# Plain fp32 products in a Hyena convolution, and other homes, later sums and longer lags around it

## The chip, the cores and the metric

The kernel runs on one core of a Trainium2 chip. The metric is the device time of one execution in microseconds (us), the median of three runs. The profile is of one execution more, whose own time is given beside its span.

## The reference

Two layers of a diffusion backbone over 1024 latent tokens and 256 context tokens, width 1024, all in fp32. Layer 0's mixer is a gated linear attention beside a grouped-query attention. Layer 1's is a Hyena convolution of order 2 on 512 channels beside a differential attention. Each mixer and each MLP sits between a pre-norm with a modulated shift and scale, and a post-norm, a gate and a residual add. Cut to what matters here:

```python
def sq_relu_mlp(h, w1, w2):
    return jnp.square(jax.nn.relu(h @ w1)) @ w2        # 1024 -> 4096 -> 1024
# Hyena: z = v; for each of two orders: z = x_o * long_conv(z, filter_o)
#   (filters for both directions over 1024 positions, computed from a small network)
# modulation: c @ w_ada gives shift, scale and gate of each sub-layer
```

## The kernel before

TensorE works on 128x512 blocks. Most products of fp32 data are made as three reduced ones: a helper `split` (L92) copies a block on ScalarE into a reduced `hi` (L94) and subtracts it on VectorE, or on GpSimd, into `lo` (L95), and `mm3` (L98) adds hi*hi, hi*lo and lo*hi (L103, L104, L105). Some, as the transposes and the attention's `o_ps` (L2244), are plain fp32 calls.

The program is written as generators that are woven together, and the framework plans from it each engine's order ahead of time: an instruction may be placed long before its place in the program where its inputs are ready. Each engine and each DMA queue runs its own order, so one that waits holds all behind it. Tiles live in pools, whose layout decides which earlier tile's memory a new one takes, and so for what a load has to wait.

**The convolution** (`hy_conv`, L1945) is a Fourier transform of 1024 rows in four residues r, in the order 0, 2, 1, 3. For each order o: `forward` makes per residue, for each of two matrices (kt), two product chains `fa_ps` of two terms; `take` combines them on VectorE (L1967, L2026) and ScalarE (L2019); `spectrum` multiplies with the filter's transform on VectorE, some 40 operations of 128x1024 for each kt; `backward` makes per residue two chains `y_ps` of four terms and multiplies them into z (L1973); for o = 0 the forward of the next order is interleaved with it. At the end z is stored to `hy` (L2108). The 32 matrices `hm` come over GpSimd's queue (L1993), z over SyncE's (L2002). Ahead of a product chain, `parts` splits z (`hz_`) or a spectrum block (`hb`).

The convolution runs as `side()` beside the differential attention, and what is left of it after that in a loop (L2506 on) with two fillers: `wo_rest`, which splits output weights on GpSimd, and `half`, half of the output projection of the attention's rows (`ho_t` L1111 transposes, `ho_lo`, `ho_ps`, `ho_o`), which is advanced by `due`, a rate per step of the spectrum (steps that yield 2). `half` has 16 block products of four triples each; what is not done in the loop runs behind it. The next step (`mlp_in`) reads `hy` as `y_in` for transposes `tr_ps` (L1155).

**The down projection** (`mlp_down`, L1425) multiplies by a Strassen-like scheme of seven products p1 to p7 over 16 steps k each; a step is four row blocks of three reduced products into `dn_ps` (L1526 to L1528). `load(i)` brings `dn_h` and `dn_b` (the first two steps over ScalarE's queue, later ones over SyncE's), `prep` makes differences and splits two steps ahead, `put` adds a finished product into the accumulators (`accx`, `accy`, L1507) at k = 15. In p5 the block `dn_t` is kept for later steps. With the context (layer 0) there are two more accumulators `accz`. `ends` is the post-norm, gate and residual (L1067, L1071, L1072) of finished rows, and what follows them, one stage per `next`.

**The modulation** (`ada_halves`, L237) loads `w_ada`, makes eight scaled sums `ada_acc` per stream and half on VectorE (L261), splits the sum into `ada_hl` on ScalarE and GpSimd, and after `lag` yields sums it over the partitions on TensorE (`ada_ps`, L277). It is woven into the first projection at L577 and into the qk columns of layer 1 at L2479 at a rate per step of these; what a rate leaves over runs behind the main loop.

Of the kernel before, what the change touches and what calls it, by code (L numbers as in the profile page):

```python
# [8 lines left out]
F32 = mybir.dt.float32  # L9
# [455 lines left out]
def in_proj0(g, ps, ftp, vgp):  # L465
# [11 lines left out]
    with ExitStack() as st:  # L477
# [96 lines left out]
            run(first)  # L574
        pq.append(st.enter_context(g.tc.tile_pool(name="ip_q", bufs=1, reuse_waits="tile")))
        bg = st.enter_context(g.tc.tile_pool(name="ip_bg", bufs=1, reuse_waits="tile"))
        for n, _ in enumerate(woven(pipelined(items), (ada_halves(g, bg, [(0, j) for j in AJ], 1), 1.3))):  # L577
            if n == 12:
                wts = vg_weights(g, ft, 0)
                vg = vg_columns(g, ft, vgp(), wts)  # L580
            if n >= 20:
                for _ in range(2):
                    next(vg)
# [841 lines left out]
def mlp_down(g, layer, ap, pool, x_src, bg, rates, after, group, bufs):  # L1425
# [22 lines left out]
    zs = [two(ap, f"accz{t}") for t in range(2 if ctx else 0)]  # L1448
    st = ExitStack()
    rp, p = (st.enter_context(g.tc.tile_pool(name=f"{n}{layer}", bufs=1, reuse_waits="tile")) for n in ("dr", "dn"))  # L1450
    raws, parts, cs, gates = {}, {}, {}, []
    where = dict(p1=(0, 0), p2=(1, 0), p3=(1, 1), p5=(0, 1)) if ctx else {}

    def pair(name, shape, bufs):
# [2 lines left out]
    def load(i):  # L1457
        if i >= len(steps):
            return
        n, k = steps[i]  # L1460
        q = nc.scalar if i < 2 else nc.sync
        h = rp.tile([128, 512], F32, name="dn_h", bufs=bufs[0])
        q.dma_start(out=h, in_=g.hid[k][n])
        ws = []
        for b in DOWN_W[n]:
            if n == "p5" and b == "b12":
                w = ts[k] = p.tile([128, 512], F32, name=f"dn_t{k}")
            else:
                w = rp.tile([128, 512], F32, name="dn_b", bufs=bufs[1])
            r0, c0 = k * 256 + (int(b[1]) - 1) * 128, (int(b[2]) - 1) * 512  # L1470
            q.dma_start(out=w, in_=w2[r0:r0 + 128, c0:c0 + 512])
            ws.append(w)
        c = None
        if n in where:
            c = p.tile([128, 2, 256], FR, name="dn_c", bufs=bufs[2])
            nc.sync.dma_start(out=f(c), in_=g.hid_c[k][:, where[n][0]])
        raws[i] = h, ws, c
# [31 lines left out]
    def put(n, t, ps):  # L1509

        x, y = xs[t], ys[t]
        if n in ("p1", "p3", "p5"):
            nc.scalar.copy({"p1": y[:, 0], "p3": x[:, 1], "p5": y[:, 1]}[n], ps)
            return
        add(x[:, 0] if n == "p2" else y[:, 0], ps, y[:, 0])
        if n == "p6":
            add(x[:, 1], x[:, 1], y[:, 1])
            add(x[:, 1], x[:, 1], y[:, 0])
        elif n == "p7":
            add(y[:, 1], y[:, 1], y[:, 0])  # L1520

    def terms(ps, i, t, sums=nb):
        (hh, hl), (wh, wl) = parts[i][0:2]
# [46 lines left out]
    for i, (n, k) in enumerate(steps[:len(steps) - group]):  # L1570
        due += rates.get(n, 0)
        while due >= 1.0:
            next(bg, None)
            due -= 1.0
        prep(i + LA)
        if k == 0:
            ps = tiles(4)
            if n in ("p1", "p3") and ctx:
                cps = [psa(g, [128, 512], name="dc_ps", tag="cx") for _ in range(2)]
            if n == "p7":  # L1580
                run(bg)
                gates.extend(mod(g, pool, layer, 5, range(2 - layer), name="gate", tag="gate", bufs=2))
        for t in range(4):
            terms(ps[t], i, t)
            if k == nb - 1:
                put(n, t, ps[t])
        if n in where:
            context(i, cps)
        del parts[i]
        if n in ("p7", "p4") and k % 2:  # L1590
            next(ends, None)
    run(ends)
    last = range(len(steps) - group, len(steps))
# [351 lines left out]
def hy_conv(g, pool):  # L1945
# [1 line left out]

    nc = g.nc
    g.hy = g.dram.tile([1024, HY], F32, name="hy")
    RS = (0, 2, 1, 3)
# [35 lines left out]
    def load_mat():  # L1989
        if todo:  # L1990
            src, i, j = todo.pop(0)
            m = pool.tile([128, 2, 2, 2, 128], FR, name="hm", bufs=3)
            nc.gpsimd.dma_start(out=m.rearrange("p a b w k -> p (a b w k)"), in_=g.i[src][i, j])  # L1993
            mats.append(m)

    def matrix():
# [1 line left out]
        return mats.pop(0)  # L1998

    def load_z(j, r):  # L2000
        z = tile2("hz", 2)
        nc.sync.dma_start(out=z, in_=rows(g.hv[j], r))  # L2002
        return z

    def parts(z, name, bufs):
        hi, lo = (tile2(name + x, bufs, FR) for x in ("hi", "lo"))
        split(g, hi, lo, z)
        return hi, lo

    def forward(r, z, A):  # L2010

        hi, lo = z

        def take(kt, c, ps):
            a = A[kt]
            if r < 2:
                if c == 0:
                    a["d", r] = tile2("hw", 8)
                nc.scalar.copy(a["d", r][:, c], ps)  # L2019
                return  # L2020
            i = r - 2
            if c == 0:
                a["s", i] = tile2("hw", 8)
            d = a["d", i][:, c]
            add(a["s", i][:, c], ps, d)
            nc.vector.scalar_tensor_tensor(d, ps, -1.0, d, op0=ALU.mult, op1=ALU.add)  # L2026

        for kt in range(2):
            m = matrix()
            for c in range(2):  # L2030
                ps = psa(g, [128, HY], name="fa_ps", tag="hy")
                mm3(g, ps, [(m[:, c, j, 0], m[:, c, j, 1], hi[:, j], lo[:, j]) for j in range(2)])
                flush()
                later.append(lambda kt=kt, c=c, ps=ps: take(kt, c, ps))
                yield 1
# [59 lines left out]
    def backward(o, r, A, made):  # L2095

        z = load_z(1 + o, r)
        bs = [parts(A[kt][r], "hb", 3) for kt in range(2)]
        yield 1

        def take(jt, ps):
            mul(z[:, jt], ps, z[:, jt])
            if jt == 0:
                return
            if o == 0:
                made[r] = z
            else:
                nc.sync.dma_start(out=rows(g.hy, r), in_=z)  # L2108

        for jt in range(2):  # L2110
            m = matrix()
            ps = psa(g, [128, HY], name="y_ps", tag="hy")
            mm3(g, ps, [(m[:, kt, c, 0], m[:, kt, c, 1], bs[kt][0][:, c], bs[kt][1][:, c])
                        for kt in range(2) for c in range(2)])
            flush()
            later.append(lambda jt=jt, ps=ps: take(jt, ps))
            yield 1
# [1 line left out]
    for _ in range(2):  # L2119
        load_mat()  # L2120
    A = [{}, {}]
    zs = [load_z(0, r) for r in RS[:2]]
    for i, r in enumerate(RS):
        z = parts(zs[i], "hz_", 1)
        if i + 2 < 4:
            zs.append(load_z(0, RS[i + 2]))
        yield 1
        yield from forward(r, z, A)
    flush()
    for o in range(2):  # L2130
        for kt in range(2):
            yield from spectrum(o, kt, A[kt])
        zs, nxt, z = {}, [{}, {}], None
        for i, r in enumerate(RS):
            yield from backward(o, r, A, zs)
            if o == 0:
                if z:
                    yield from forward(RS[i - 1], z, nxt)
                flush()
                z = parts(zs.pop(r), "hz_", 1)  # L2140
        flush()
        if o == 0:
            yield 1
            yield from forward(RS[3], z, nxt)
            flush()
        A = nxt
# [247 lines left out]
def tile_kernel(ctx, tc, ins, out):  # L2394
# [57 lines left out]
    with st:  # L2452
# [23 lines left out]
        wt, raw = w_block(g, w_load(g, w, 2048), None, True), w_load(g, w, 1536)  # L2476
        cbp = pool_of(hold, "cb", "right")
        with tc.tile_pool(name="qkc", bufs=1, reuse_waits="tile") as pool:
            bg = ada_halves(g, pool, ADA[1:])  # L2479
            df_rows = diff_rows(g, pool)  # L2480
            for n, _ in enumerate(woven(qk_columns(g, ft, pool, wt, raw), (bg, 0.4))):
                if n == 60:
                    raw, raw1 = (w_load(g, w, c, cbp) for c in (0, 128))
                if n == 66:
                    wt = w_block(g, raw, cbp)
    y1d = [g.dram.tile([128, HY], F32, name=f"y1d_{t}") for t in range(NT)]
    wo = ExitStack()
    with ExitStack() as st:
# [14 lines left out]
        with tc.tile_pool(name="ho1", bufs=1, reuse_waits="tile") as pool:  # L2503
            half = proj_half(g, w, range(4, KT), range(NC_T, NT), lambda t: y1d[t], pool, True, 0, keep)
            for _ in range(4):
                next(half)  # L2506
            rest = wo_rest(g, w, range(4), keep, True, 0)
            due = 0.0
            for n, kind in enumerate(hyena):
                if n % 16 == 8:  # L2510
                    next(rest, None)
                due += 0.33 if kind == 2 else 0.0
                if due >= 1.0:
                    next(half, None)
                    due -= 1.0
            run(rest)
            run(half)
# [18 lines left out]
def _consts():  # L2536
# [42 lines left out]

    r, kt, p, im, jt, k = np.ix_(*(np.arange(n) for n in (4, 2, 128, 2, 2, 128)))  # L2580
    m = turns(kt * 128 + k, 4 * (jt * 128 + p) + r, im)
    c["k_df"] = np.ascontiguousarray(parts(m)).reshape(4, 2, 128, 1024)

    r, jt, k, kt, im, p = np.ix_(*(np.arange(n) for n in (4, 2, 128, 2, 2, 128)))
    m = turns(kt * 128 + k, 4 * (jt * 128 + p) + r, im) / 1024
    c["k_di"] = np.ascontiguousarray(parts(m)).reshape(4, 2, 128, 1024)

    im, b, kt, x, p, s, k = np.ix_(*(np.arange(n) for n in (2, 2, 2, 2, 128, 4, 128)))
    m = turns(kt * 128 + k + 512 * b, 2 * (s * 128 + p) + x, im)
# [21 lines left out]
```

## Time and profile before

| | us |
|---|---|
| median of three runs | 3460.94 |
| the runs | 3454.71 to 3467.56 |
| the profiled execution, its own time | 3455.77 |
| its span | 3454.0 |

How to read the rows: PE is TensorE's products, PEld its weight loads, DVE VectorE, ACT ScalarE, POOL GpSimd, SP SyncE; a name with q is the engine's DMA queue. Times are us from the start of the span, mean durations ns. In a row of the waits, what stands before the arrow waited for what stands behind it. In a row of a stretch stand its bounds, its length, the busy time of PE, PEld, DVE, ACT and POOL with the number of instructions, the granted clock of TensorE as a share of full speed, the DMA engines' busy share and GB/s. In the order of time, "x2" puts together instructions of one line that follow each other.

### The profile page before, as it was taken

What the parts mean: (1) busy time and instruction counts of PE and PEld (TensorE: products, weight loads), DVE (VectorE), ACT (ScalarE), POOL (GpSimd) and SP (SyncE); (2) the same over time, 40 slices, a digit from 0 to 9 for tenths busy, and PEclk for the clock granted to TensorE, in tenths of its full rate; (3) what the DMA queues carried; (4) which work ended last, traced back from release to release, by engine and by line L of the source; (5) the groups of instructions that cost most, each with busy time, mean ns of one, the idle gap of its engine ahead of it and who ended that gap; (6) DMA issues with size and microseconds to landing.
All of it is one profiled execution on the core that took longest, in us unless ns stands there. A gap on an engine that the chain in (4) does not pass through costs nothing.

```text
span 3454.0 us, 42343 instructions
## 1 busy us (share of the span) xinstructions
PE 3130.1 (91%) x13936; PEld 2437.8 (71%) x13936; DVE 2612.2 (76%) x4530; ACT 1562.4 (45%) x3174; POOL 742.6 (22%) x540
## 2 busy tenths in 40 slices
PE   8888899889987999989998899999848789999998
PEld 4766677567766788878876777776536667887886
DVE  6788998878658776767688665778798589877776
ACT  4444766555555222223345543677532352224443
POOL 0254655523321222101110122100030112210000
PEclk9999999899998999999999999999979899999999
DMA  6544111477753334378777365332445635438954
GB/s 225 151 128 140 49 43 42 135 215 219 256 198 107 131 134 144 130 263 292 234 244 252 104 196 170 103 84 60 139 154 168 224 105 190 140 137 301 316 188 150
DMA packets 346632, 575.10 MB, mean 167 GB/s; under 512 B 43329, under 2 KB 138561, under 8 KB 346284
## 3 DMA queue, kind: packets, MB, share of 16 engines
q1 hardware_dynamic: 296244, 491.17, 43.7%
q10 hardware_dynamic: 40952, 47.67, 4.0%
q0 software_dynamic: 9216, 33.56, 3.5%
q8 instruction: 110, 1.80, 0.2%
q14 instruction: 110, 0.90, 0.1%
HBM read 418.74 MB, written 153.54 MB: 166 GB/s over the span
## 4 chain that ended last, share of the span: by engine, by line
PE 57%; DVE 22%; DMA 7%; issue 6%; ACT 4%; POOL 3%; SPq 0%; ACTq 0%; POOLq 0%; DVEq 0%
PE up_ps L105 5%; PE up_ps L104 5%; PE up_ps L103 5%; PE dn_ps L1527 5%; PE dn_ps L1526 5%; PE dn_ps L1528 5%; DVE gq_lo L95 3%; DVE gq_mx L732 2%; PE s_ps L637 2%; PE o_ps L2244 1%; PE up_ps L1245 1%; DVE ada_acc L261 1%; PE pj_ps L104 1%; PE pj_ps L103 1%; PE pj_ps L105 1%
## 5 line engine op out<-in xcount | busy, mean ns | idle before, releaser
L1526 PE MATMUL dn_ps<-dn_w_hi,dn_h_hi 128*128 128x512 f32 x896 | 352.3, 395 | 30.6 <-DVE accy L1507 17.0
L1527 PE MATMUL dn_ps<-dn_w_lo,dn_h_hi 128*128 128x512 f32 x896 | 353.8, 395 | 4.9 <-DVE dn_w_lo L95 4.7
L1528 PE MATMUL dn_ps<-dn_w_hi,dn_h_lo 128*128 128x512 f32 x896 | 352.6, 394 | 0.0
L95 POOL TENSOR_TENSOR w_lo<-up_w,w_hi 128x512 fp32r<-128x512 f32 x106 | 145.9, 1386 | 579.5 <-ACT w_hi L94 565.5
L94 ACT ACTIVATE dn_h_hi<-dn_h 128x512 fp32r<-128x512 f32 x224 | 140.8, 629 | 278.3 <-PE dn_ps L1527 193.0
L95 DVE TENSOR_TENSOR dn_h_lo<-dn_h,dn_h_hi 128x512 fp32r<-128x512 f32 x224 | 162.6, 726 | 80.4 <-ACT dn_h_hi L94 80.0
L1526 PEld LDWEIGHTS dn_ps<-dn_w_hi,dn_h_hi 128*128 128x128 f32 x896 | 170.4, 190 | 71.2 <-DVE accy L1507 19.0
L765 POOL TENSOR_TENSOR gq_acc<-gq_acc,gq_p 128x512 f32<-128x512 f32 x128 | 183.9, 1437 | 87.4 <-ACT gq_p L754 83.9
L1527 PEld LDWEIGHTS dn_ps<-dn_w_lo,dn_h_hi 128*128 128x128 f32 x896 | 170.5, 190 | 44.1 <-DVE dn_w_lo L95 8.6
L1528 PEld LDWEIGHTS dn_ps<-dn_w_hi,dn_h_lo 128*128 128x128 f32 x896 | 170.4, 190 | 35.3
L95 DVE TENSOR_TENSOR gq_lo<-gq_p,gq_hi 128x512 fp32r<-128x512 f32 x168 | 177.5, 1068 | 20.0 <-ACT gq_hi L94 19.6
L261 DVE SCALAR_TENSOR_TENSOR ada_acc<-w_ada,sc,ada_acc 128x512 f32<-128x512 f32 x224 | 172.7, 808 | 19.9 <-DMA w_ada<-in_w_ada 19.2
L95 POOL TENSOR_TENSOR ada_hl<-ada_acc,ada_hl 128x512 fp32r<-128x512 f32 x32 | 63.9, 2007 | 512.4 <-ACT ada_hl L94 443.0
L94 ACT ACTIVATE s_hi<-up_w 128x512 fp32r<-128x512 f32 x128 | 79.2, 630 | 195.8 <-DVE up_w L1234 122.5
L103 PE MATMUL up_ps<-t_hi,s_hi 128*128 128x512 f32 x384 | 153.0, 398 | 2.0 <-ACT t_hi L94 1.3
L105 PE MATMUL up_ps<-t_hi,s_lo 128*128 128x512 f32 x384 | 152.7, 399 | 2.2 <-DVE s_lo L95 2.2
L1234 DVE TENSOR_TENSOR up_w<-up_w 128x512 f32<-128x512 f32 x128 | 92.3, 724 | 81.4 <-POOL w_lo L95 79.6
L104 PE MATMUL up_ps<-t_lo,s_hi 128*128 128x512 f32 x384 | 152.7, 398 | 1.1 <-DVE t_lo L95 1.1
L647 DVE TENSOR_REDUCE sm_m<-s_ps 128x1 f32<-128x512 f32 (+1 forms) x192 | 110.7, 596 | 43.8 <-PE s_ps L637 42.6
L661 ACT ACTIVATE df_p<-s_ps,sm_m 128x512 f32<-128x512 f32 (+1 forms) x192 | 116.9, 620 | 39.8 <-DVE sm_m L651 37.2
L754 ACT ACTIVATE gq_p<-st_ps 128x512 f32<-128x512 f32 x168 | 99.4, 597 | 73.0 <-PE st_ps L752 55.6
L94 ACT ACTIVATE w_hi<-up_w 128x512 fp32r<-128x512 f32 x106 | 64.6, 628 | 148.4 <-DMA up_w<-in_w_mlp_in 68.3
(512 smaller groups left out, 9198.9 us busy)
## 6 DMA issues: line engine op xcount, KB each, us to landing
dn_b<-in_w_mlp_out SPq DMA_DIRECT2D x252, 256.0 KB
w_ada<-in_w_ada SPq DMA_DIRECT2D x96, 512.0 KB
up_w<-in_w_mlp_in SPq DMA_DIRECT2D x32, 1024.0 KB
hy_m<-in_k_ff POOLq DMA_DIRECT2D x32, 512.0 KB, 5.7
dn_c<-hidc SPq DMA_DIRECT2D x64, 256.0 KB
x<-x_in SPq DMA_DIRECT2D x26, 512.0 KB
x_in<-x SPq DMA_DIRECT2D x26, 512.0 KB
cb_raw<-in_od_w_in SPq DMA_DIRECT2D x20, 512.0 KB
```

Of the source, the lines that this page charges most:

```text
L94: g.nc.scalar.activation(hi, src, ACTF.Copy)
L95: (g.nc.gpsimd if pool else g.nc.vector).tensor_tensor(lo, src, f(hi), op=ALU.subtract)
L103: nc.tensor.matmul(out, ah, bh, start=(i == 0), stop=False)
L104: nc.tensor.matmul(out, ah, bl, start=False, stop=False)
L105: nc.tensor.matmul(out, al, bh, start=False, stop=(i == n - 1))
L261: nc.vector.scalar_tensor_tensor(acc[:, s], w[:, k], sc, acc[:, s], op0=ALU.mult, op1=ALU.add)
L647: nc.vector.tensor_reduce(m[:, i:i + 1], s, axis=AX.X, op=ALU.max)
L661: g.nc.scalar.activation(d, s, ACTF.Exp, bias=m, scale=0.125, accum_out=l[:, i:i + 1])
L765: nc.gpsimd.tensor_tensor(sums[u], sums[u], p, op=ALU.add)
L1526: nc.tensor.matmul(ps, hh[:, sl], wh, start=(k == 0), stop=False)
L1527: nc.tensor.matmul(ps, hh[:, sl], wl, start=False, stop=False)
L1528: nc.tensor.matmul(ps, hl[:, sl], wh, start=False, stop=(k == nb - 1))
```

## The change

Five things are changed together. In the convolution the products are plain fp32 calls on unsplit blocks: `products` takes the place of `mm3`, the splits fall away, a matrix is 256 KB instead of 512 KB (the constants `k_df` and `k_di` are made in one part, not two), there are four `hm` buffers instead of three and four `hz` instead of two, all four first z loads are issued at the start, and twelve `yield 1` fall away. The rate of `half` goes from 0.33 to 0.28. In layer 0's down projection the 16 `dn_t` tiles are allotted first in the pool of the raw loads, ahead of `dn_h` and `dn_b`. The sums of p6 and p7 that need no fresh product are put off, two per step, and `ends` advances at every step of p7 from k = 5 and of p4, not at every second. The modulation's lag goes from 1 to 2 in the first projection, with rate 1.4 for 1.3, and from 1 to 3 in the qk columns.

```diff
@@ first projection, modulation beside it
-        for n, _ in enumerate(woven(pipelined(items), (ada_halves(g, bg, [(0, j) for j in AJ], 1), 1.3))):
+        for n, _ in enumerate(woven(pipelined(items), (ada_halves(g, bg, [(0, j) for j in AJ], 2), 1.4))):
@@ mlp_down
-    raws, parts, cs, gates = {}, {}, {}, []
+    raws, parts, gates, later = {}, {}, [], []
+    if ctx:
+        ts = {k: rp.tile([128, 512], F32, name=f"dn_t{k}") for k in range(nb)}
@@ load
             if n == "p5" and b == "b12":
-                w = ts[k] = p.tile([128, 512], F32, name=f"dn_t{k}")
+                if not ctx:
+                    ts[k] = p.tile([128, 512], F32, name=f"dn_t{k}")
+                w = ts[k]
@@ put
         if n == "p6":
-            add(x[:, 1], x[:, 1], y[:, 1])
-            add(x[:, 1], x[:, 1], y[:, 0])
+            later.append((x[:, 1], y[:, 1]))
+            later.append((x[:, 1], y[:, 0]))
         elif n == "p7":
-            add(y[:, 1], y[:, 1], y[:, 0])
+            later.append((y[:, 1], y[:, 0]))
+
+    def flush(most):
+        for _ in range(min(most, len(later))):
+            d, x = later.pop(0)
+            add(d, d, x)
@@ the loop over the steps
         prep(i + LA)
+        flush(2)
@@
-        if n in ("p7", "p4") and k % 2:
+        if n == "p7" and k > 4 or n == "p4":
             next(ends, None)
@@ hy_conv: load_mat, load_z
-            m = pool.tile([128, 2, 2, 2, 128], FR, name="hm", bufs=3)
-            nc.gpsimd.dma_start(out=m.rearrange("p a b w k -> p (a b w k)"), in_=g.i[src][i, j])
+            m = pool.tile([128, 2, 2, 128], F32, name="hm", bufs=4)
+            nc.gpsimd.dma_start(out=m.rearrange("p a b k -> p (a b k)"), in_=g.i[src][i, j])
@@
-        z = tile2("hz", 2)
+        z = tile2("hz", 4)
@@
-    def parts(z, name, bufs):
-        hi, lo = (tile2(name + x, bufs, FR) for x in ("hi", "lo"))
-        split(g, hi, lo, z)
-        return hi, lo
+    def products(ps, terms):
+        for i, (m, x) in enumerate(terms):
+            nc.tensor.matmul(ps, m, x, start=(i == 0), stop=(i == len(terms) - 1))
@@ forward
-                mm3(g, ps, [(m[:, c, j, 0], m[:, c, j, 1], hi[:, j], lo[:, j]) for j in range(2)])
+                products(ps, [(m[:, c, j], z[:, j]) for j in range(2)])
@@ backward
-        bs = [parts(A[kt][r], "hb", 3) for kt in range(2)]
-        yield 1
+        bs = [A[kt][r] for kt in range(2)]
@@
-            mm3(g, ps, [(m[:, kt, c, 0], m[:, kt, c, 1], bs[kt][0][:, c], bs[kt][1][:, c])
-                        for kt in range(2) for c in range(2)])
+            products(ps, [(m[:, kt, c], bs[kt][:, c]) for kt in range(2) for c in range(2)])
@@ the first loads
-    zs = [load_z(0, r) for r in RS[:2]]
+    zs = [load_z(0, r) for r in RS]
     for i, r in enumerate(RS):
-        z = parts(zs[i], "hz_", 1)
-        if i + 2 < 4:
-            zs.append(load_z(0, RS[i + 2]))
-        yield 1
-        yield from forward(r, z, A)
+        yield from forward(r, zs[i], A)
@@ between backward and the next forward
-                z = parts(zs.pop(r), "hz_", 1)
+                z = zs.pop(r)
@@ main: qk columns, half projection
-            bg = ada_halves(g, pool, ADA[1:])
+            bg = ada_halves(g, pool, ADA[1:], 3)
@@
-                due += 0.33 if kind == 2 else 0.0
+                due += 0.28 if kind == 2 else 0.0
```

## Rows read from the trace of the kernel before

**Rows 1.** Page, part 1: engine, busy us, share, instructions.

```profile
PE 3130.1 (91%) x13936; PEld 2437.8 (71%) x13936; DVE 2612.2 (76%) x4530; ACT 1562.4 (45%) x3174; POOL 742.6 (22%) x540
```

**Rows 2.** TensorE's waits, whole span: line, releaser, us in total, times, longest.

```profile
PE ho_t L1111 <- DMA ho_y<-y1d: 44.9, 2, 44.6
PE dn_ps L1526 <- DVE accy L1507: 17.0, 3, 9.4
PE y_ps L104 <- DVE hblo L95: 9.0, 3, 6.1
```

**Rows 3.** Stretches of the convolution: engines' busy us, clock, DMA share, GB/s.

```profile
2447.00:2491.00 44.00, 41.30 (x178) 30.70 (x179) 34.57 (x80) 25.13 (x63) 3.71 (x7) 0.96 0.53 159
2491.00:2562.00 71.00, 20.12 (x78) 10.60 (x77) 68.74 (x92) 17.56 (x36) 6.93 (x3) 0.65 0.38 118
2562.00:2616.50 54.50, 51.02 (x206) 39.06 (x205) 36.86 (x35) 19.86 (x24) 24.45 (x21) 0.95 0.73 221
2616.50:2680.00 63.50, 48.56 (x195) 36.89 (x193) 62.90 (x76) 14.61 (x23) 0.53 (x1) 0.89 0.43 140
2680.00:2705.50 25.50, 22.51 (x85) 17.74 (x86) 13.45 (x15) 4.24 (x4) 2.65 (x5) 0.87 0.66 206
2705.50:2730.00 24.50, 14.50 (x52) 11.38 (x51) 7.93 (x11) 6.74 (x12) 4.97 (x4) 0.72 0.90 300
```

**Rows 4.** Groups by line, 2447 to 2720: busy us, mean ns, idle before.

```profile
L103 PE MATMUL y_ps<-hbhi,hm 128*128 128x512 f32 x64 | 26.5, 416 | 3.0 <-DMA hm<-in_k_di 1.9 <-ACT hbhi L94 0.8 <-ACT ho_o L1121 0.2
...
L103 PE MATMUL fa_ps<-hz_hi,hm 128*128 128x512 f32 x64 | 26.3, 421 | 3.1 <-ACT hz_hi L94 2.6 <-DMA hm<-in_k_df 0.5
...
L95 DVE TENSOR_TENSOR hblo<-ht,hbhi 128x1024 fp32r<-128x1024 f32 x8 | 14.5, 1812 | 2.2 <-ACT hbhi L94 2.2
...
L95 DVE TENSOR_TENSOR hz_lo<-hz,hz_hi 128x1024 fp32r<-128x1024 f32 x8 | 9.7, 1218 | 8.4 <-ACT hz_hi L94 8.3
```

**Rows 5.** Order of time on TensorE: start, us busy, [idle before, releaser].

```profile
2426.25 1.02 PE L2244 MATMUL o_ps<-pt,dvT 128*128 128x512 f32 x2
...
2427.35 0.40 PE L1667 MATMUL hc_ps<-ftx_lo,cb_hi 128*128 128x512 f32 x1
...
2440.18 1.92 PE L2244 MATMUL o_ps<-pt,dvT 128*128 128x512 f32 x2
...
2701.13 0.40 PE L103 MATMUL y_ps<-hbhi,hm 128*128 128x512 f32 x1
...
2704.35 0.39 PE L105 MATMUL y_ps<-hbhi,hm 128*128 128x512 f32 x1
...
2717.67 1.94 PE L1155 MATMUL tr_ps<-ident,y_in 128*128 128x128 f32 x8 [7.44 <-DMA y_in<-hy]
```

**Rows 6.** Order of time at layer 0's down start, ScalarE's queue and TensorE.

```profile
1497.49 0.35 ACTq L1463 DMA_DIRECT2D dn_h<-hid_0p  x1
...
1504.62 0.79 PE L1526 MATMUL dn_ps<-dn_w_hi,dn_h_hi 128*128 128x512 f32 x1 [11.03 <-ACT dn_w_hi L94]
```

**Rows 7.** TensorE's waits, 3115 to 3135 (layer 1's down start).

```profile
PE dn_ps L1527 <- DVE dn_w_lo L95: 4.3, 1, 4.3
```

**Rows 8.** Order of time on VectorE around p6's end, layer 0.

```profile
1816.67 2.48 DVE L1071 SCALAR_TENSOR_TENSOR accz<-accz,rs_t,gate 128x1024 f32<-128x1024 f32 x2 [3.52 <-DMA gate<-mods]
...
1835.14 1.28 DVE L1507 TENSOR_TENSOR accy<-dn_ps,accy 128x512 f32<-128x512 f32 x2
```

**Rows 9.** Order of time on TensorE at p7's end, layer 1.

```profile
3397.72 0.79 PE L1526 MATMUL dn_ps<-dn_w_hi,dn_h_hi 128*128 128x512 f32 x1 [5.29 <-DVE accy L1507]
```

**Rows 10.** TensorE's waits, 2030 to 2090 (two rows), then 100 to 220.

```profile
PE ada_ps L277 <- ACT ada_hl L94: 7.0, 3, 4.4
PE ada_ps L277 <- POOL ada_hl L95: 1.6, 2, 0.8
...
PE ada_ps L277 <- POOL ada_hl L95: 4.1, 3, 2.4
```

**Rows 11.** Page, part 5: the modulation's sums on VectorE.

```profile
L261 DVE SCALAR_TENSOR_TENSOR ada_acc<-w_ada,sc,ada_acc 128x512 f32<-128x512 f32 x224 | 172.7, 808 | 19.9 <-DMA w_ada<-in_w_ada 19.2
```

More of the change, by code (lines that the diff above doesn't have):

```diff
@@ L2000, in load_z @@
     def load_z(j, r):
-        z = tile2("hz", 2)
+        z = tile2("hz", 4)
         nc.sync.dma_start(out=z, in_=rows(g.hv[j], r))
         return z
-    def parts(z, name, bufs):
-        hi, lo = (tile2(name + x, bufs, FR) for x in ("hi", "lo"))
-        split(g, hi, lo, z)
-        return hi, lo
+    def products(ps, terms):
+        for i, (m, x) in enumerate(terms):
+            nc.tensor.matmul(ps, m, x, start=(i == 0), stop=(i == len(terms) - 1))
     def forward(r, z, A):
-        hi, lo = z
         def take(kt, c, ps):
@@ L2581, in _consts @@
     m = turns(kt * 128 + k, 4 * (jt * 128 + p) + r, im)
-    c["k_df"] = np.ascontiguousarray(parts(m)).reshape(4, 2, 128, 1024)
+    c["k_df"] = np.ascontiguousarray(m.astype(f4)).reshape(4, 2, 128, 512)
     r, jt, k, kt, im, p = np.ix_(*(np.arange(n) for n in (4, 2, 128, 2, 2, 128)))
     m = turns(kt * 128 + k, 4 * (jt * 128 + p) + r, im) / 1024
-    c["k_di"] = np.ascontiguousarray(parts(m)).reshape(4, 2, 128, 1024)
+    c["k_di"] = np.ascontiguousarray(m.astype(f4)).reshape(4, 2, 128, 512)
     im, b, kt, x, p, s, k = np.ix_(*(np.arange(n) for n in (2, 2, 2, 2, 128, 4, 128)))
```

## The prediction

> **What bounds the kernel now.** I read the page's totals first. TensorE is busy 91% of the span and VectorE 76% [rows 1], so the span is mostly TensorE's, with stretches in which another engine ends last. A change here pays only where TensorE stands still or runs slowly, so the second view is its waits over the whole run, grouped by what released them [rows 2]. Three of them touch the diff: 44.9 us in the convolution for `ho_t`, 17.0 us at the MLP's `dn_ps` for VectorE's sums (`accy`), and 9.0 us of `y_ps` for split halves. Third, a table of the convolution by stage [rows 3]. It reads: forward of order 0 beside attention, 2447 to 2491 (TensorE 41.30 of 44.00); spectrum of order 0 to 2562 (VectorE 68.74 of 71.00, TensorE mostly idle, so its 44.9 us wait is hidden behind VectorE); backward 0 with forward 1 to 2616.5 (TensorE 51.02 of 54.50); spectrum 1 to 2680 (VectorE 62.90 of 63.50); backward 1 to 2705.5 (TensorE 22.51 of 25.50); the way out to 2730 at a granted clock of 0.72. So two stages are VectorE's and three TensorE's. The waits in the MLP and the modulation stand singly and are read below, from the order of time and from the waits of short windows.
>
> **The plain products (convolution).** A triple of reduced products becomes one plain fp32 product, 64 in `fa_ps` and 64 in `y_ps` [rows 4]. The reduced ones start 3.22 us apart over 14, so 0.23 each and 0.69 a triple [rows 5]. The other plain product of this shape, attention's L2244, is recorded as two instructions per call: from its start at 2426.25, with one reduced product between, to the next at 2427.35 is 1.10 us, less 0.23 is 0.87. So each replacement costs TensorE +0.17 to +0.18 us, and 128 cost +22 us if every one is on the path. What the same edit takes off: 24 splits, of which the three rows are 14.5, about as much again for the other eight of `hb`, and 9.7 us on VectorE [rows 4], so 38 us, and a like number of ScalarE copies; half of the matrices' bytes; and the reuse wait of the two z buffers, now four. Here a rule stands against the change. The row has 0.87 us against 0.69. The Trainium skill, "FP8 and Floating Point Precision", section "TensorE Precision Notes", says that true fp32 takes four passes through the array; four passes at one row's 0.23 would be 0.92 us, an estimate, and +29 us in place of +22, with -20 for the sum below in place of -27. The trace agrees nearly (0.87 is 3.8 times 0.23), and the sum goes by the row.
>
> By stage, with +0.17 a product:
> Forward 0: 32 products, +5.5, against 2.7 us of TensorE idle time that the splits' loss can close. Taken +2 (0 to +5.5).
> Spectrum 0: VectorE's; one split of 1.2 us falls out. Taken -1 (-5, if the first products start at once on its end, to 0).
> Backward 0: 64 products, +11; the 9.0 us for `hblo` go [rows 2], as no split is left to wait for, and with the lower rate (0.33 to 0.28, and fewer yields to count) some five half-projection triples of 0.69, 3.5 us, move to later stages. Taken -2 (-9 to +11).
> Spectrum 1: two splits of 1.2 us fall out of a full VectorE; the half-projection there is hidden on TensorE. Taken -2 (-3 to 0).
> Backward 1: 25 triples fall into it, +4.3, against 3.0 us idle and a clock of 0.87. Taken 0 (-4 to +4.3).
> Way out: before, two half-projection products are left, TensorE idles 7.44 us [rows 5] and then works at 0.72. At 0.28 over about 41 counted yields 11 of 16 are done and five remain, 5 x 4 triples x 0.69 = 13.7 us, which is more than the 13.1 us from 2704.58 (the last `y_ps` start, 2704.35, and 0.23) to 2717.67. They fill the gap and run a little over. Taken -3 (-6 to +3).
> Sum -6; the ends add to -27 and +24, of which I keep -20 and +14, since not all fall one way.
>
> **Other homes (layer 0's down projection).** The first `dn_h` and `dn_b` loads reuse memory that the up projection's last stores read, so their issue on ScalarE's queue stands at 1497.49, behind the end of up, and TensorE idles 11.03 us to 1504.62 [rows 6]. Sixteen `dn_t` tiles put first in that pool move those loads 32 KB up, over tiles that by my layout of the pools are freed 14 to 20 us earlier. Behind the waiting issue on ScalarE's queue stand the second step's loads and then the splits themselves. The steps from the third on load over SyncE behind up's last stores and stay late. Layer 1 shows what is left of such a start where the loads are free: its longest wait there is 4.3 us, for `dn_w_lo` [rows 7]. Taken 11.0 - 4.3 = -7. Ends: -13 (with the slow clock after the wait) and 0 (the loads wait for another tile).
>
> **Put-off sums and later ends.** `flush(2)` takes eight adds in p6 and four in p7 out of the burst behind a product's last step. In layer 0 at p6 to p7 the chain is: `accz` waits 3.52 us for `gate` from `mods`, everything on VectorE stands behind it, and the sums come at 1835.14 [rows 8], 9.4 us late for TensorE (the longest of the 17.0). The put-off does not remove that by itself: two of the burst's adds, 2.5 us, are what it moves. The start of the ends at k > 4 rather than k = 1 can, if the ends' `accz` is then not placed ahead of p6's sums. I give that four in ten: 0.4 x 11 (9.4 and the slow products after it) is 4.4, with a little for the burst -5. Ends: -11, 0. At p7 to p4 the remaining 17.0 - 9.4 = 7.6 us stand in two layers, the larger 5.29 before 3397.72 [rows 9]. VectorE is full up to there, so half a burst less gives little, and the ends now run in every step of p4, which asks more of it. Taken -2 (-6 to +4).
>
> **Longer lags (modulation).** TensorE waits 7.0 us for ScalarE's half of `ada_hl` in the qk columns and 4.1 us for GpSimd's in the first projection [rows 10]. With lag 3 the halves have two more steps of the columns to come; all 7.0 should go, with the 1.6 us for GpSimd beside it. The price: 32 yields are wanted and about 72 x 0.4 = 29 given, so three run behind the columns, uncovered: two sums of 0.81 us each (the page's 808 ns) [rows 11], so 3 x 1.6 = +4.8. In the first projection lag 2 at rate 1.4 should hide most of 4.1: -3.2. Sum -8.6 + 4.8 - 3.2 = -7. Ends: -15 (the late steps are covered, the clock stays up) and +3 (the waits move to the next row).
>
> **Sum.** -6 - 7 - 5 - 2 - 7 = -27 us. The profiled execution took 3455.77 (span 3454.0), the median of the runs is 3460.94, 5.2 above it. So 3455.8 - 27 = 3428.8, and 3434 on the median's scale.
>
> **Rivals.**
> Only homes and lags pay. The engines' order is planned over the whole program, and the same work may be placed as before: the sums stay late, the convolution gains nothing on VectorE's stages and loses what it gains on TensorE's. Then -7 and -7 are left, with +2 for the burst's adds spread over a full VectorE: -12, 3449. For it: VectorE at 68.74 of 71.00 and 62.90 of 63.50 hardly loses work. Against it: 9.0 us of `hblo` waits end with the splits.
> The products become the bound (the other side). Plain products stand on the path in three stages, +22, and many run at the lower clock: at 2440.18 the pair took 1.92 us for 1.02 [rows 5], so 0.87 becomes about 1.65, 0.8 more. Backward 0 begins after 45 us of idle TensorE and backward 1 behind a VectorE stage; 20 products at that clock are +16. The convolution then costs +38, the rest gives -21: +17, 3478. It decides from +21 in the convolution, where the rest is just eaten. Against it: TensorE's idle time in these stages, 2.7, 3.5 and 3.0 us, is there to close, and dense plain products hold it busy longer than triples with gaps.
> All of it comes, with the clock: homes -13, sums -11 and -5, lags -13, convolution -8: -50, 3411. For it: after each of these waits the products start at the lower clock (0.79 us at 1504.62 and 3397.72, against 0.39). Against it: each must find its cover.
>
> **How the numbers follow.** Chances: forecast 0.46 (its own range 3419 to 3448), only homes and lags 0.22, products bound 0.16, all of it 0.16. The range reaches from 3404 to 3472: it leaves out the lower third of the last case and the upper half of the third. I call 0.5%, 17.3 us, what a measurement can tell from no change: faster is below 3443.6, slower above 3478.2. Faster: 0.85 of the first, 0.3 of the second, all of the last, 0.62. Slower: half of the third and a little, 0.09. Same: 0.29.
>
> **What would show it.** Right: `fa_ps` and `y_ps` as 256 records at some 0.43 us spacing and no `hz_` or `hb` splits; backward 0 no longer than 54 us; TensorE busy from 2704 to the way out; the wait before layer 0's down under 4 us; `accz` behind p6's sums; no `ada_hl` waits in the qk columns. Wrong: a plain product over 0.9 us at full clock, backward 0 at 60 us or more, `dn_h` still issued behind up's last store, or a wait on the ends in p4.

## The result and the profile after

The changed kernel takes 3444.52 us in the median of five runs (3442.42 to 3446.22), the one before 3463.15 in the runs beside it. The ratio is 0.9946, 95% interval 0.9927 to 0.9964: 18.6 us faster. That is 0.54%, just over the 0.5% that I called measurable, with an interval that reaches down to 0.36%; the line of 3443.6 that I drew from the first median (3460.94) is missed by 0.9 us. Run again beside three experiments the changed kernel gave 0.9953 (0.9941 to 0.9966). The profiled execution took 3444.68 us, 11.1 less than that of before (3455.77), so the traces show less of a gain than the medians.

The page's totals, part 1:

```profile
PE 3149.4 (91%) x13808; PEld 2411.9 (70%) x13808; DVE 2577.8 (75%) x4506; ACT 1535.4 (45%) x3150; POOL 745.1 (22%) x540
```

TensorE is busy 19 us longer than in [rows 1], in a span 11 us shorter. This total is not the price of the plain products: with the convolution's part alone (e1, below) it rises by 1.9 only, to 3132.0. TensorE's waits over the whole span, as in [rows 2]:

```profile
PE y_ps L2016 <- DVE ht L1976: 24.3, 3, 13.3
...
PE dn_ps L1535 <- DVE accy L1511: 18.7, 3, 9.0
...
PE dn_ps L1536 <- DVE dn_w_lo L95: 9.3, 6, 4.3
PE dn_ps L1535 <- ACT dn_w_hi L94: 8.9, 3, 8.4
...
PE ada_t L290 <- DVE ada_rows L282: 7.0, 2, 4.2
...
PE ada_t L290 <- DVE ada_rows L280: 5.4, 3, 3.5
```

Of `ho_t`'s 44.9 us 3.5 are left, and the 9.0 for `hblo` are gone; `y_ps` now waits 24.3 us for the spectrum itself (`ht`). The waits for `accy` did not shrink (18.7 for 17.0). `dn_w_hi` still costs 8.9 and `dn_w_lo` 9.3 (12.7 and 4.7 before), and `ada_t` waits 12.4 us for its rows (4.3 before).

**Where the time went.** Starts of the first or last product of a name in the order of time on TensorE, before, and the difference to it (us) after and in four experiments. A column that stays level loses nothing in that stretch. Each column is one trace, and a landmark by itself says little: e8, the changed kernel once more, has +5.70 at the first `dn_ps` where this trace has +8.83, and e4, which edits nothing ahead of it, has +5.06 at the first `up_ps`. So a step counts here where several traces share it.

| start of | before | after | conv alone (e1) | +projection (e5) | +qk (e6) | +down (e7) |
|---|---|---|---|---|---|---|
| layer 0, first `up_ps` | 1020.73 | +8.98 | +0.26 | +6.69 | +3.10 | -0.05 |
| layer 0, first `dn_ps` | 1504.62 | +8.83 | +0.49 | +6.12 | +1.47 | -2.54 |
| last `dc_ps` (end of p5) | 1781.40 | +12.60 | -0.71 | +5.62 | +1.62 | +3.91 |
| first `qk_ps` | 2009.02 | +16.24 | +1.62 | +10.11 | +4.33 | +8.58 |
| first `cv_ps` | 2145.36 | +23.15 | +1.54 | +9.32 | +12.16 | +8.83 |
| last `cv_ps` | 2436.15 | +22.15 | +2.30 | +8.26 | +12.57 | +9.87 |
| first `fa_ps` | 2447.74 | +7.52 | -12.33 | -6.37 | -2.06 | -4.77 |
| first `y_ps` | 2562.33 | -26.27 | -45.91 | -40.36 | -36.04 | -38.72 |
| last `tr_ps` (way out) | 2814.80 | -10.86 | -30.55 | -22.29 | -18.10 | -23.10 |
| last `dn_ps` | 3441.71 | -11.10 | -36.12 | -25.27 | -20.19 | -25.73 |

So the changed kernel loses 9.0 us up to layer 0's MLP, 7.4 from the first `dn_ps` to layer 1's first `qk_ps`, 6.9 in the qk columns, and gains 34.0 from there to the last `tr_ps` (23.15 to -10.86).

The stretches of the convolution after, columns as in [rows 3]; bounds put at the same events (forward 0, spectrum 0, backward 0, spectrum 1, backward 1, way out):

```profile
2455.00:2499.00 44.00, 44.00 (x154) 24.04 (x153) 31.30 (x77) 23.26 (x61) 3.77 (x7) 1.00 0.41 135
2499.00:2562.40 63.40, 37.70 (x116) 17.91 (x115) 63.29 (x95) 18.59 (x43) 0.54 (x1) 0.76 0.31 100
2562.40:2609.00 46.60, 45.49 (x106) 19.82 (x105) 15.48 (x24) 10.61 (x14) 26.57 (x23) 1.00 0.60 197
2609.00:2669.60 60.60, 46.58 (x183) 32.99 (x182) 60.53 (x73) 10.02 (x18) 0.54 (x1) 0.93 0.41 139
2669.60:2690.30 20.70, 20.70 (x48) 9.04 (x46) 6.77 (x11) 0.00 (x0) 2.15 (x4) 0.94 0.41 127
2690.30:2719.00 28.70, 23.69 (x97) 18.16 (x96) 9.41 (x13) 9.12 (x16) 5.06 (x4) 0.88 0.83 261
```

Backward 0 takes 46.6 us against the 58.3 between the same two events before (2560.39, the last `ht` of spectrum 0, to 2618.70, the first of spectrum 1); backward 1 takes 20.7 against 26.5 (2678.09 to 2704.58). TensorE is full in both. Why backward 0 is shorter stands in the order of time on TensorE:

```profile
2531.29 0.66 PE L2258 MATMUL ot_ps<-ident,o_sb 128*128 128x128 f32 x4 [0.68 <-ACT o_sb L2250]
2536.06 6.75 PE L2016 MATMUL y_ps<-ht,hm 128*128 128x512 f32 x8 [4.12 <-DVE ht L1976]
2542.65 3.60 PE L2016 MATMUL y_ps<-hw,hm 128*128 128x512 f32 x8
2559.56 5.25 PE L2016 MATMUL y_ps<-ht,hm 128*128 128x512 f32 x8 [13.31 <-DVE ht L1976]
2564.65 3.60 PE L2016 MATMUL y_ps<-hw,hm 128*128 128x512 f32 x8
2568.08 7.03 PE L2016 MATMUL fa_ps<-hz,hm 128*128 128x512 f32 x16
```

16 instructions, eight plain products, run at 2536 to 2546 within spectrum 0, and the next from 2559.56, as its last `ht` comes out. Eight of the stage's 64 are out of the way before it begins, and the other 56 at 0.86 us are 48 us, about its length. Before, the first `y_ps` started at 2562.33, and 23 of the half-projection's reduced products (8.5 us busy) stood among them.

### The profile page after: what moved, and what is told of

Its sections match the earlier page's. It is cut to its first block, busy times and chain, and to the rows that moved or that the text cites. A ratio compares the mean times of both kernels' runs of the same rounds, so it can differ in the third digit from the quotient of the medians.

```text
span 3442.9 us, 42047 instructions
## 1 busy us (share of the span) xinstructions
PE 3149.4 (91%) x13808; PEld 2411.9 (70%) x13808; DVE 2577.8 (75%) x4506; ACT 1535.4 (45%) x3150; POOL 745.1 (22%) x540
## 5 line engine op out<-in xcount | busy, mean ns | idle before, releaser
L1535 PE MATMUL dn_ps<-dn_w_hi,dn_h_hi 128*128 128x512 f32 x896 | 352.3, 395 | 28.9 <-DVE accy L1511 18.7
L95 DVE TENSOR_TENSOR dn_h_lo<-dn_h,dn_h_hi 128x512 fp32r<-128x512 f32 x224 | 158.8, 709 | 68.5 <-ACT dn_h_hi L94 68.1
```

What stands on the lines that cost most here:

```text
L95: (g.nc.gpsimd if pool else g.nc.vector).tensor_tensor(lo, src, f(hi), op=ALU.subtract)
L1535: nc.tensor.matmul(ps, hh[:, sl], wh, start=(k == 0), stop=False)
```

## The experiments

Twelve runs, each timed against the kernel before. The ratios are given with 95% intervals, and a gain in us without further words is the ratio's share of 3463.

**e1, the convolution's part alone** (the convolution's hunks of the diff and the rate 0.28, nothing else).

> The convolution's part alone (plain products, four z and matrix buffers, no split yields, rate 0.28). By the landmarks of the two traces (what each stretch gained or lost): about -33 us, all between the attention's projections and the end of the output projection, nothing ahead of 2400. By the prediction's term: -6 us, with forward 0 no earlier. If the products were the bound: +10 to +20.

0.9891 (0.9876 to 0.9905), 3420.98 us: -38, or -40 by the medians, faster than the changed kernel by 19 by the ratios and 24 by the medians. The landmarks' reading holds and my term of -6 does not.

**e2, the projection's lag alone; e3, the qk columns' lag alone; e4, homes, sums and ends alone.**

```diff
# e2
-  (ada_halves(g, bg, [(0, j) for j in AJ], 1), 1.3)
+  (ada_halves(g, bg, [(0, j) for j in AJ], 2), 1.4)
# e3
-  bg = ada_halves(g, pool, ADA[1:])
+  bg = ada_halves(g, pool, ADA[1:], 3)
```

> The modulation's lag 2 and rate 1.4 in the first projection alone. By the landmarks: -7 us by the end of the projection and then +16 in the attention and filter work behind it, +9 in all. By the prediction's term: -3 us. A third reading, that the loss behind the projection comes from some other part through the plan of the whole program: the -7 stay, nothing is lost later.

> Lag 3 in the qk columns of layer 1 alone. By the landmarks: +5 us, lost between the first qk_ps and the first cv_ps, because three modulation steps run behind the columns. By the prediction's term: -4 us (-8.6 of waits, +4.8 of late steps).

> The down projection's parts alone (homes, put-off sums, ends). By the landmarks: 0 at layer 0's start, +4 to +7 by layer 0's end, -2 in layer 1, so about +3 us. By the prediction's terms: -14 us (-7 homes, -5 and -2 sums and ends).

1.0007 (0.9996 to 1.0017), 1.0007 (0.9999 to 1.0016), 1.0000 (0.9991 to 1.0009). None of the three gains. By the times alone none is clearly a loss either; the landmarks' losses come again in each trace. In e2 the last product of attention's `l_ps` is 6.9 us late (6.4 to 10.3 in the kernels with this lag at rate 1.4, -1.0 to +0.4 in those without it) and the first `up_ps` 4.9, no more than e4's 5.1 there. e3 goes from +4.51 at the first `qk_ps` to +11.21 at the first `cv_ps`, e4 from +0.09 at the first `dn_ps` to +7.09 at the first `qk_ps`. So they were added to the convolution's part.

**e5, e6, e7: e1 with each of the three; e8: the changed kernel again.**

> The convolution's part with the first projection's lag and rate. The convolution alone gave -39 us, the projection's part alone +2. If parts add: about -36. If the two stand in each other's way (one planned order for the whole program), the stretch between the projection and layer 0's up costs more with both than with the lag alone (+5 at its first up_ps): up to +14, and about -25 in all.

> The convolution's part with lag 3 in the qk columns. If parts add: about -36 (-39 and +2). If the late modulation steps meet the convolution's earlier start beside attention: -30 or less of a gain, the loss between qk_ps and the end of attention.

> The convolution's part with the down projection's parts. If parts add: about -39 (-39 and 0). If the down projection's later order loses by the other placing of memory: +7 between layer 0's first dn_ps and the qk columns, so about -32.

> The changed kernel once more, in the rounds of the three before it. If its 18.6 us of gain stand: about -19, so the parts together lose 18 us that none of them loses alone. If that was the run: -30 to -38.

0.9901 (0.9887 to 0.9914), 0.9922 (0.9908 to 0.9935), 0.9907 (0.9894 to 0.9921), 0.9953 (0.9941 to 0.9966). Against e1 they lose 0.10, 0.31 and 0.16%, together 0.57%, and 0.9891 + 0.0057 = 0.9948 is the changed kernel. On the convolution's base the parts add; the places are those of the table. Only e6's interval lies clear of e1's; the other two losses rest on the table as much as on the times.

In e6, the order of time on TensorE at the end of the qk columns:

```profile
2132.72 0.63 PE L277 MATMUL ada_ps<-ada_hl,colsr 128*1 128x512 f32 x2
...
2137.53 0.58 PE L290 MATMUL ada_t<-ident,ada_rows 1*128 1x1 f32 x4 [4.19 <-DVE ada_rows L282]
```

The last modulation step runs at 2132.72, behind the columns, and its transposes wait 4.19 us for the row's two VectorE operations; everything of the next stage stands behind them.

**e9, e1 with the twelve yields put back; e10, before with the twelve yields dropped and nothing else.**

```diff
# e9, on e1 (backward, first loads)
         bs = [A[kt][r] for kt in range(2)]
+        yield 1
...
     for i, r in enumerate(RS):
+        yield 1
         yield from forward(r, zs[i], A)
# e10, on before
         bs = [parts(A[kt][r], "hb", 3) for kt in range(2)]
-        yield 1
...
-        yield 1
         yield from forward(r, z, A)
```

> The convolution's part with the twelve dropped yields put back (products plain, buffers and rate as changed). If forward 0's earlier start beside attention comes from the dropped yields: first fa_ps 8 to 12 us later than with them dropped, and about -27 in all. If it comes from the products and loads (no splits to wait for): first fa_ps within 4 us of the convolution alone, and about -36.

> Before with the twelve yields dropped and nothing else: split products, old buffers, old rate. If the pace alone brings the start: first fa_ps 8 to 12 us earlier, -10 in all. If the splits hold the start: within 4 us, and 0 in all. In either case y_ps stays behind the splits, and backward 0 takes its 58 us.

0.9940 (0.9917 to 0.9964) and 0.9963 (0.9948 to 0.9978). So plain products with the old pace (and the rate 0.28, which was not run alone) give -21 us, the new pace with split products -13, both -38. The intervals are 5 to 8 us to either side, so that both together give more than the sum is read from the traces, not from the times. The start of the convolution goes with the products: first `fa_ps` against last `cv_ps` is +11.6 before, -3.0 in e1, -3.1 in e9, +8.8 in e10. Most of it is the first z load. On SyncE's queue, its issue and its wait before, then in e1:

```profile
2436.88 8.21 SPq L2002 DMA_DIRECT2D hz<-hv  x2
SPq L2002 <- DVE hy_cv L1710: 11.2, 1, 11.2
...
2425.71 5.52 SPq L2002 DMA_DIRECT2D hz<-hv  x4
SPq L2002 <- PE hc_ps L1668: 3.5, 1, 3.5
```

Before and in e10 the load waits 11.2 us for `hy_cv`, an operation on the convolution's filters; in e1 and e9 it does not, and goes out ahead of the last `cv_ps`. So no data ties it to them, and the wait is read as one for memory that `hy_cv` held; which of the changed buffers moved the load's home was not taken apart. Against the last `cv_ps` the load moves by 13.5 us, and the remaining 1.1 of the 14.6 is the split ahead of the first product. Backward 0 needs both the products and the pace. In e9, TensorE's order:

```profile
2550.04 1.97 PE L1111 MATMUL ho_t<-ident,ho_y 128*128 128x128 f32 x8 [42.84 <-DMA ho_y<-y1d]
...
2555.20 1.02 PE L2007 MATMUL y_ps<-ht,hm 128*128 128x512 f32 x2
```

With the old pace more of the spectrum's steps fall behind attention, where they advance `half` (this is read from the program), and its `ho_t` stands ahead of `y_ps` with a wait of 42.84 us. Backward 0 takes 59.0 us (2551.39 to 2610.37). In e10 the pace puts `y_ps` first, but the splits hold it:

```profile
2522.19 1.22 PE L103 MATMUL y_ps<-hbhi,hm 128*128 128x512 f32 x2 [5.51 <-ACT hbhi L94]
2543.29 0.80 PE L104 MATMUL y_ps<-hblo,hm 128*128 128x512 f32 x1 [19.88 <-DVE hblo L95]
...
2551.56 0.50 PE L104 MATMUL y_ps<-hblo,hm 128*128 128x512 f32 x1 [3.03 <-DVE hblo L95]
```

One pair runs early, then TensorE waits 19.88 us for `hblo`, which VectorE makes in its full order, and again 3.03. Backward 0 takes 61.6 us (2548.48 to 2610.05). Together the rows answer it: the plain product needs no VectorE work between spectrum and TensorE, and the pace lets it be first.

**e11, e1 with the other homes, old sums and ends, and the first loads on GpSimd's queue.**

```diff
-        q = nc.scalar if i < 2 else nc.sync
+        q = nc.gpsimd if i < 4 and ctx else nc.scalar if i < 2 else nc.sync
```

> The convolution's part, the other homes alone (old sums and ends), and the loads of layer 0's first four down steps issued on GpSimd's queue instead of ScalarE's and SyncE's. If the homes are free and the order on ScalarE and SyncE holds the loads: first dn_ps 6 to 11 us earlier than with the convolution alone, the wait for dn_w_hi under 3 us, and about -46 in all. If memory still holds them: the wait stays at 8 to 11 us and about -39. If the homes by themselves cost the later steps of layer 0 (as the loss of 7 us before the last dc_ps may say): that loss shows again, without the sums and ends.

0.9889 (0.9870 to 0.9908), 3420.15 us: as e1. The first `dn_ps` comes 10.0 us earlier than in e1, and by the last `dc_ps` all but 0.6 of it is lost. GpSimd's queue, TensorE and VectorE in order of time:

```profile
1474.97 0.61 POOL L1465 DMA_DIRECT2D dn_h<-hid_0p  x1 [8.05 <-PE up_ps L105]
...
1495.15 1.18 PE L1530 MATMUL dn_ps<-dn_w_hi,dn_h_hi 128*128 128x512 f32 x2 [3.72 <-ACT dn_w_hi L94]
...
1501.84 0.49 DVE L259 TENSOR_SCALAR ada_acc<-w_ada,sc 128x512 f32<-128x512 f32 x1 [6.54 <-DMA w_ada<-in_w_ada]
1502.24 0.68 DVE L95 TENSOR_TENSOR dn_w_lo<-dn_b,dn_w_hi 128x512 fp32r<-128x512 f32 x1
...
1502.98 0.80 PE L1531 MATMUL dn_ps<-dn_w_lo,dn_h_hi 128*128 128x512 f32 x1 [6.66 <-DVE dn_w_lo L95]
```

The first load goes out at 1474.97, 20 us ahead of its use; the first wait falls to 3.72. Then VectorE stands 6.54 us at a modulation sum that waits for `w_ada`, the split `dn_w_lo` stands behind it, and TensorE waits 6.66 us for that. 3.72 and 6.66 together come near e1's single wait of 11.30.

**e12, e1 with both lags and rates that pay for the added yields** (lag 2 at 1.8, lag 3 with 0.5 for 0.4).

> The convolution's part with both longer lags, and rates that make up for the added yields: 1.8 in the first projection (1.3 and 1.4 before), 0.5 in the qk columns (0.4 before). If the lags lose because their added yields put modulation steps behind the main loops: the last ada_t of the first projection is earlier than 290, layer 0's first up_ps no later than with the convolution alone, the last cv_ps no later either, and about -39 to -50 in all. If the lag only moves the wait from ada_ps to ada_t, or the attention behind loses for another reason: up_ps still +5 to +7, cv_ps still +8 or more, and about -25.

0.9933 (0.9916 to 0.9949). From first `up_ps` to last `cv_ps` the trace loses nothing (+7.89 to +7.36; e6 +3.10 to +12.57): the qk loss was the late steps. For the first projection the theory fell: its last `ada_t` is early (283.51, before 291.59), and still first `up_ps` is at +7.89. There the projection itself is slower at this rate: the first `vg_ps` is 12.9 us later than before, where lag 2 at 1.4 (e5) had it 6.0 earlier.

## Why the prediction was right or wrong

The time lies in the range and the sign was right, but by luck: the convolution gave 28 us more than its term, the other parts cost 44 us more than theirs, and the two errors cancelled in part. The time lies nearer to the rival "only homes and lags pay" (3449) than to the forecast (3434), with the opposite mechanism: only the convolution paid. Of the signs named, the convolution's four came; those of the other parts did not (8.40 us before layer 0's down projection, `accz` ahead of p6's sums, 3.1 us of `ada_hl` waits left in the qk columns).

| term | predicted | traces, after against before |
|---|---|---|
| convolution | -6 | -34.0 |
| homes | -7 | -0.2 from the first `up_ps` to the first `dn_ps`, +3.8 from there to the end of p5 |
| sums, ends | -7 | +3.6 from there to the first `qk_ps` (their own waits, `accy`: +1.7) |
| lags | -7 | +9.0 projection and what follows, +6.9 qk |
| sum | -27 | -11 |

**The products' price was right.** After, 16 records last 7.03 us, so (7.03 - 0.59)/15 = 0.43 each, with 0.59 the busy time of a single such record, and 0.86 a product; 0.87 was forecast. By the four passes that the Trainium skill gives for true fp32 ("FP8 and Floating Point Precision", "TensorE Precision Notes") I had made 0.92; the trace lies below it. All records of `fa_ps` and `y_ps` together are busy 120.3 us for 102.4, and 118.9 in e1: +16.5 to +17.9 against +22.

**Forward 0 (+2) and spectrum 0 (-1).** The sum forgot that the stage's start was free to move: `fa_ps` starts 14.6 us earlier against `cv_ps` (+11.6 to -3.0). I priced the products in a fixed window, not what stands ahead of the first one, the z load's wait of 11.2 us; the stage itself, from the first `fa_ps` to the first `ht` of spectrum 0, is as long as before (43.5 us for 43.1). Spectrum 0 lasts 63.6 us (2498.76 to 2562.36) for 69.6 (2490.82 to 2560.39), 62.5 in e10 and 67.0 in e9, so this part comes mostly with the pace; why is not shown.

**Backward 0 (-2).** The step "the 9.0 us for `hblo` go" put these waits into the wrong stage. They stand in the trace of before at 2672.83, 2681.16 and (0.8 us) 2700.55, at the end of spectrum 1 and in backward 1:

```profile
2672.83 0.80 PE L104 MATMUL y_ps<-hblo,hm 128*128 128x512 f32 x1 [6.09 <-DVE hblo L95]
...
2681.16 0.80 PE L104 MATMUL y_ps<-hblo,hm 128*128 128x512 f32 x1 [2.13 <-DVE hblo L95]
```

The wait that counted for backward 0 was hidden: behind `ho_t`'s 44.9 us stood products that could have run in VectorE's stage. I had called that wait hidden because VectorE set the end; it was, and work placed into it came off the next stage: -11.7. The rival "products become the bound" did come true as to the stage (TensorE 45.5 us of 46.6 in it), and it is shorter all the same. Its lower clock came too, at 2536: the first eight records took 6.75 us, the next eight 3.60. But that was in VectorE's stage, and backward 0 itself has a granted clock of 1.00 (0.95 before, [rows 3]).

**Spectrum 1 (-2).** From its first to its last `ht` it takes 60.6 us (2609.03 to 2669.65) for 59.4 (2618.70 to 2678.09): the splits that fell out gave nothing there.

**Backward 1 (0), way out (-3).** -5.8, as the splits between spectrum and product fell (21.0 us in e9, which has plain products and the old pace, 25.2 in e10, which has splits and the new one); and +3.5 on the way out (2704.58 to 2814.80 is 110.2, after 2690.26 to 2803.94 is 113.7), where the products of `half` do fill the gap, as forecast, and hold it a little longer (the 13.7 us that I gave five of them are 13.8 by their own terms, which changes nothing).

**Homes (-7).** The step that failed is that memory held the loads. In order of time on ScalarE's queue, TensorE and VectorE after:

```profile
1507.25 0.42 ACT L94 ACTIVATE up_c<-up_r 128x256 fp32r<-128x256 f32 x1 [1.80 <-DVE up_r L1250]
1507.28 0.33 ACTq L1465 DMA_DIRECT2D dn_h<-hid_0p  x1
...
1513.45 0.80 PE L1535 MATMUL dn_ps<-dn_w_hi,dn_h_hi 128*128 128x512 f32 x1 [8.40 <-ACT dn_w_hi L94]
...
1516.47 0.88 DVE L259 TENSOR_SCALAR ada_acc<-w_ada,sc 128x512 f32<-128x512 f32 x2 [8.34 <-DMA w_ada<-in_w_ada]
1517.27 0.69 DVE L95 TENSOR_TENSOR dn_h_lo<-dn_h,dn_h_hi 128x512 fp32r<-128x512 f32 x1
```

`dn_h` goes out 0.03 us behind `up_c`, the last copy of up: ScalarE's own order holds it. Before, it went out 1.69 us behind `up_c` (1495.80), so memory held it by less than 2 us. TensorE's first wait fell from 11.03 [rows 6] to 8.40, and then VectorE stands 8.34 us for `w_ada` ahead of the split, and `dn_w_lo` costs 3.9 more. The pair comes again in every kernel with these homes and loads on ScalarE's queue (8.4, then 3.6 in e4, 3.7 in e7 and 3.9 in e8). p1, from its first `dn_ps` to p2's, takes 72.5 us for 68.5: what the first wait gave, 2.6, the next took back with more. e11 took the queue away and met the same modulation sum. That this sum is the last holder is read from the rows; a run with `w_ada` loaded earlier was not made.

**Sums and ends (-5, -2).** VectorE at p6's end in layer 0, as in [rows 8]:

```profile
1827.90 1.28 DVE L1071 SCALAR_TENSOR_TENSOR accz<-accz,rs_t,gate 128x1024 f32<-128x1024 f32 x1 [2.49 <-DMA gate<-mods]
...
1846.16 0.69 DVE L1492 TENSOR_TENSOR dn_b<-dn_b 128x512 f32<-128x512 f32 x1 [2.50 <-DMA dn_b<-in_w_mlp_out]
...
1847.37 2.48 DVE L1511 TENSOR_TENSOR accy<-dn_ps,accy 128x512 f32<-128x512 f32 x4
```

`accz` still runs ahead of p6's sums and waits 2.49 us for `gate`; the sums come as late for TensorE (9.0 us, 9.4 before). The six in ten that I gave this happened. The chain had one more holder that I did not name: right ahead of the sums VectorE waits 2.50 us for `dn_b`, a raw weight of p7 (2.91 before, at 1833.93). At p7's end layer 0 waits 6.1 (2.4 before), layer 1 3.6 (5.3 before, [rows 9]); in all `accy` costs 1.7 us more. The +3.6 from the end of p5 to the first `qk_ps` cannot be laid on these parts: e1, e5 and e6, which lack them, lose 2.3, 4.5 and 2.7 there. The loss ahead of p6 (e7: -2.54 to +3.91) is the homes': the put-off sums act only from p6 on, and it is in every kernel with the homes (3.8 to 8.1 us from the first `dn_ps` to the end of p5; e11, without sums and ends, has the largest) and in no other (-1.2 to +0.7).

**Lags (-7).** For the qk columns the price of +4.8 for three late steps was about right (first `qk_ps` to first `cv_ps` is +6.9), and the gain of 8.6 was wrong: the wait went from `ada_ps` to `ada_t`. From e1 to e6 the first falls from 9.7 to 3.4 us, the second rises from 1.2 to 10.2. I had that only as a bound. For the first projection the gain came (first `vg_ps` -6.8), and was lost in attention behind it: its last `l_ps` is 10.3 us late (676.3 for 666.0), and the projection's columns that fill it (`vg_ps`) run out at 592.59 instead of 625.35. That they run out early is seen in e2 and e5 as well; that this is the cause is not shown, and in e12, where they last to 649.21, `l_ps` is 5.7 us late all the same. It stays open.

The best version is e1 (or e11, the same time): the change without its other four parts.

## What to carry to other kernels

A wait that another engine hides is still room: ask which later work could run in it and what stands between, an engine's order or a helper operation on the full engine. When a diff has several parts, price each stage from the event that releases its first instruction, not within the window that the old trace gives it. A longer lag in a woven generator adds yields; unless the rate pays for them, its last steps move behind the main loop, onto the path. A wait that moves a stage's start can stand on a queue that the views of the busy engines do not show, as the z load's on SyncE's.

## What the runs showed that was not expected

Twelve dropped yields, which do no work, are worth 13 us with split products (e10) and 17 with plain ones (0.9940 to 0.9891, e9 to e1). With plain ones 12.2 of it is backward 0 (59.0 us to 46.7 in the traces), because they decide which of two stages' work stands first on TensorE; with split ones backward 0 is 3.3 us longer, and spectrum 0 gives 7.0. The same load costs GpSimd 0.61 us of its time to issue in e11, and ScalarE's queue 0.35 [rows 6].
